# Two-layer hybrid attention kernel: each query tile's scores, the transposes of the tile ahead of it and the value products as one row on TensorE, held in program order between the weight products

## The chip, the cores and the metric

One core of a Trainium2 chip runs the whole program; the other cores stay idle. The metric is the device time of one execution in microseconds. Times of runs below are medians; the trace comes from one profiled execution.

## The reference

Two layers of a diffusion backbone work on 256 latent tokens and 256 context tokens of width 1024, all in fp32:

```python
for l in range(DEPTH):
    x = x + 0.5 * m[2] * swiglu(modulate(x, ...), w1, w3, w2)          # and the same for the context h
    o_lat, o_ctx = mixer(modulate(x, ...), modulate(h, ...), w_in[l], ...)
    x = x + m[5] * (o_lat @ w_out[l])
    x = x + 0.5 * m[8] * swiglu(modulate(x, ...), ...)                 # context too, in layer 0 only
return rms_norm(x, final_g)
```

The mixer projects the input once and feeds three groups of heads: a gated linear recurrence in both directions (4 heads), a neighbourhood attention with a bias per head (6 heads), and a windowed attention with rotary positions and a sink per head (6 heads that share 2 key heads). Each attention is `softmax(q @ k.T * scale + bias) @ v` over 256 latent and 256 context keys. Context queries see the 256 context keys alone, and only layer 0 has them.

## The kernel before, in words

**Products.** Weights are split into a high and a low part (line 109 on ScalarE, line 110 on VectorE), and `mm3` (line 237) makes three matmuls of each 128x128 weight block: high by high, low by high, high by low, all recorded at line 227. Activations lie transposed, so a product has up to 512 columns (both token sets) in layer 0 and 256 (latent alone) for most of the last layer.

**Attention.** `attention` (line 891) runs over *units*: a head pair j and a tile of 128 queries qt. Layer 0 has 12 units for each of the two kinds ("na", the neighbourhood kind, and "sw", the windowed kind), six of them with 512 keys (qt 0 and 1) and six with 256; layer 1 has six units of 512 keys for each kind. A unit has three stages:

- `stage_s`: the scores of both heads on TensorE (line 915, tile s), then a softmax on the other engines: on VectorE bias and row minimum in one pass (line 938; for 256 keys a reduction, line 943), for sw the sink (line 946); on ScalarE the exponential with its sum (line 947) and for sw that of the sink (line 949); on VectorE the sum (950), its reciprocal (951) and the scaling of P (952).
- `stage_t`: per head, four (or two) 128x128 transposes of P on TensorE (line 960, tile pt) and one copy out of PSUM on ScalarE (line 964, tile ptsb).
- `stage_v`: for two units together, the value products on TensorE (line 981, tile ot). After the last unit of a head pair ot is split into o by both engines (lines 221 and 222).

The loop's step i traces the scores of unit i, the transposes of unit i-1, and on odd i from 3 the value products of units i-2 and i-3.

**Order of the work.** `mixer` weaves three generators by the share of a stated cost that each has used: the projections followed by `w_out` (stated 99), the recurrence (stated 170) and attention (stated 30). `w_out` makes 8 output blocks of five products (15 matmuls) from the first five o tiles, which the recurrence and na fill; `w_out_end` adds the three o tiles of sw. Each kind of attention yields 34.8 cost units in layer 0, so that after na alone the attention's share (34.8 of 30) is past all that the first generator reaches (99.3 of 99): the sw steps are traced behind all 120 matmuls of `w_out`. In layer 1 a kind yields 17.4 (0.58 of 30), while the first generator stands at 57.7 of 99 (0.58) where `w_out` begins and ends at 70.7 (0.71): there the sw steps are traced among the products of `w_out`. The traced order isn't the order on the engines: a list scheduler fills each engine's queue by priority among what it holds ready. Attention is traced under `EARLIER = -450`, a priority of earlier work, so its instructions may be placed ahead of products that were traced before them. In the kernel before, only the scores of a head pair's first tile are held, behind a mark in the projection that makes their q and k (`R.marks`), and the transposes behind the last scores traced. Each engine then works its queue strictly in the order it has been given.

Of the kernel before, what the change touches and what calls it, by code (L numbers as in the profile page):

```python
# [197 lines left out]
class Kern:  # L198
# [27 lines left out]
    def mmul(self, *args, **kw):  # L226
        ins = self.nc.tensor.matmul(*args, **kw)  # L227
        if self.pinned:
            self.tc.keep_in_program_order(ins)
        return ins  # L230
# [5 lines left out]

    def mm3(self, ps, whi, wlo, ahi, alo, start, stop):
        mmul = self.mmul
        mmul(ps, whi, ahi, start=start, stop=False)
        mmul(ps, wlo, ahi, start=False, stop=False)  # L240
        return mmul(ps, whi, alo, start=False, stop=stop)


    def plan(self):
# [646 lines left out]
    def attention(self, l, R, kind):  # L891

        nc = self.nc
        nqt = R.nq // 128
        units = [(j, qt) for j in range(3) for qt in range(nqt)]
        U = {}
        ots = {}
        last = []

        def mark(i):  # L900
            return 2 * units[i][0] + 2 if kind == "na" else 8 + units[i][0]

        def ready(i):
            return i >= len(units) or len(R.marks) > mark(i)

        def stage_s(i):

            j, qt = units[i]
            k0, nk = (0, TOK) if qt < 2 else (SEQ, SEQ)
            qs = slice(qt * 128, qt * 128 + 128)  # L910
            q, ks = R.q[kind][j], R.k[kind][j]
            pss = [self.aux("s") for _ in range(2)]
            for hh in range(2):
                hs = slice(hh * 64, hh * 64 + 64)
                ins = nc.tensor.matmul(pss[hh][:, 0:nk], q[hs, qs], ks[hh][hs, k0:k0 + nk], start=True, stop=True)  # L915
                if hh == 1:
                    self.tc.keep_in_program_order(ins)
                elif qt == 0:
                    self.behind(ins, R.marks[mark(i)])
            last.append(ins)  # L920
            for hh in range(2):
                softmax(i, hh, pss[hh])

        def softmax(i, hh, ps):
            j, qt = units[i]
            h = 2 * j + hh
            nk = TOK if qt < 2 else SEQ
            sm = self.small("sm", 32)
            nmx, tot, es, rs = (sm[:, c:c + 1] for c in range(4))
            P = self.half("P")  # L930
            if qt < 2:
                if kind == "na":
                    b = h * 2 + qt
                    bias = self.bias[:, b:13:12 - b, :]
                else:
                    bias = self.swb[:, qt:3:2 - qt, :]
                src = P
                nc.vector.tensor_tensor_reduce(out=src.rearrange("p (a b) -> p a b", a=2),  # L938
                                               in0=ps.rearrange("p (a b) -> p a b", a=2), in1=bias, scale=1.0,
                                               scalar=3e38, op0=OP.add, op1=OP.min, accum_out=nmx)  # L940
            else:
                src = ps
                nc.vector.tensor_reduce(nmx, ps[:, 0:nk], axis=AX.X, op=OP.min)
            if kind == "sw":
                sk = self.sink[:, l * 6 + h:l * 6 + h + 1]
                nc.vector.tensor_scalar(nmx, nmx, sk, None, op0=OP.min)
            nc.scalar.activation(P[:, 0:nk], src[:, 0:nk], AF.Exp, bias=nmx, scale=-1.0, accum_out=tot)
            if kind == "sw":
                nc.scalar.activation(es, sk, AF.Exp, bias=nmx, scale=-1.0)
                nc.vector.tensor_tensor(out=tot, in0=tot, in1=es, op=OP.add)  # L950
            nc.vector.reciprocal(rs, tot)
            nc.vector.tensor_scalar(P[:, 0:nk], P[:, 0:nk], rs, None, op0=OP.mult)
            U[i, hh] = P

        def stage_t(i, hh):
            nk = TOK if units[i][1] < 2 else SEQ
            P = U.pop((i, hh))
            ps = self.aux("pt")
            for c in range(nk // 128):
                ins = nc.tensor.transpose(ps[:, c * 128:c * 128 + 128], P[:, c * 128:c * 128 + 128], self.ident)  # L960
                if c == 0:
                    self.behind(ins, last[-1])
            pt = self.half("ptsb")
            nc.scalar.activation(pt[:, 0:nk], ps[:, 0:nk], AF.Copy)
            U[i, hh] = pt

        def stage_v(ii):

            first = True
            for i in ii:  # L970
                j, qt = units[i]
                k0, nk = (0, TOK) if qt < 2 else (SEQ, SEQ)
                pts = [U.pop((i, hh)) for hh in range(2)]
                if j not in ots:
                    ots[j] = self.mm("ot")
                for c in range(nk // 128):
                    tt = k0 // 128 + c
                    for hh in (1, 0):
                        h = 2 * j + hh
                        vc = (h * 64) if kind == "na" else 384 + (h // 3) * 64  # L980
                        ins = nc.tensor.matmul(ots[j][hh * 64:hh * 64 + 64, qt * 128:qt * 128 + 128],  # L981
                                               R.V[tt // 2][:, tt % 2, vc:vc + 64], pts[hh][:, c * 128:c * 128 + 128],
                                               start=c == 0, stop=c == nk // 128 - 1)
                        if not first:
                            self.tc.keep_in_program_order(ins)
                        first = False
            if max(units[i][1] for i in ii) == nqt - 1:
                n = R.nq
                o = self.slot([128, 2, 512], F32R, "o")
                self.split(o[:, 0, 0:n], o[:, 1, 0:n], ots.pop(j)[:, 0:n])  # L990
                R.o[(2 if kind == "na" else 5) + j] = o

        n = len(units)
        for i in range(n + 2):
            while not ready(i):
                yield None
            if i < n:
                stage_s(i)
                yield 1.0
            for hh in range(2):  # L1000
                if 0 <= i - 1 < n:
                    stage_t(i - 1, hh)
                    yield 0.5
            if i >= 3 and i % 2 == 1:
                stage_v((i - 2, i - 3))
                yield 1.8

    def w_out(self, l, R):
        n = R.nq
# [438 lines left out]
```

## Time and profile before

| | |
|---|---|
| runs of the kernel before | 1867.47 us median of 3 (1866.44 to 1868.5) |
| the profiled execution | 1867.86 us, of it 1866.0 us from the first to the last instruction |
| TensorE busy | 1825.9 us (98%) |
| VectorE busy | 1205.9 us (65%) |
| ScalarE busy | 717.3 us (38%) |
| granted TensorE clock, mean | 0.995 of full speed |
| chain that ended last | TensorE 91%, VectorE 4% |
| attention on TensorE | scores 144 records, transposes 240, value products 480 |

Times are us from the start of the span unless marked ns. A row of the timeline merges equal instructions that follow each other and ends, in brackets, with the time that the engine stood idle before it and whose result it waited for. Matmuls are pipelined: the step from one start to the next is the price, not the length that is shown. A fp32 matmul leaves two records, so "x32" value products are 16 of the program. Idle time of an engine that isn't the bottleneck costs nothing; idle time of TensorE here is time of the whole kernel.

### The profile page before, as it was taken

The page shows a single profiled execution, that of the slowest core. Times are in us where ns is not written, and L with a number is a line of the kernel's source. Part 1 is how long each engine was busy: PE and PEld are TensorE (multiplying, and loading weights), DVE is VectorE, ACT ScalarE, POOL GpSimd, SP SyncE. Part 2 cuts the span into 40 slices and gives each one's busy share as a digit, 9 for nine tenths or more (in the row PEclk, how much of TensorE's full clock was granted, in tenths as well). Part 3 has the DMA queues.
Part 4 walks back from the last instruction along what each step waited for, and adds up shares of the span by engine and source line. Part 5 has one row for each costly group of instructions (what it writes and reads, how often), then busy time and mean ns, then how long its engine had stood idle before and what let it go on. Part 6 is the DMA issues. An engine that isn't in the chain of part 4 may idle for free.

```text
span 1866.0 us, 27641 instructions
## 1 busy us (share of the span) xinstructions
PE 1825.9 (98%) x11071; PEld 1501.0 (80%) x11071; DVE 1205.9 (65%) x2225; ACT 717.3 (38%) x1210; POOL 123.5 (7%) x198
## 2 busy tenths in 40 slices
PE   7999999999999999999999999999999999999998
PEld 4777787789777679778778797777788977789998
DVE  4877577765864769666576685565534766677554
ACT  4422222245345665222322352132223634665443
POOL 0000000030400020000000200000001140020000
PEclk8999999999999999999999999999999999999999
DMA  9645546432211214446455334565432321246651
GB/s 350 218 158 177 171 153 201 153 132 68 69 38 43 90 32 162 157 149 210 140 166 169 119 120 152 172 211 159 147 96 85 116 66 41 67 144 202 205 170 57
DMA packets 233641, 258.23 MB, mean 138 GB/s; under 512 B 18886, under 2 KB 195370, under 8 KB 233258
## 3 DMA queue, kind: packets, MB, share of 16 engines
q1 hardware_dynamic: 233514, 256.48, 43.0%
q8 instruction: 87, 1.43, 0.3%
q14 instruction: 40, 0.33, 0.1%
HBM read 255.41 MB, written 2.48 MB: 138 GB/s over the span
## 4 chain that ended last, share of the span: by engine, by line
PE 91%; DVE 4%; ACT 1%; POOL 1%; issue 1%; DMA 0%; SPq 0%; DVEq 0%; ACTq 0%; POOLq 0%
PE mm L227 83%; PE s L915 2%; PE ot L981 2%; PE pt L960 1%; PE adaps L377 1%; DVE P L938 1%; DVE wlo L110 1%; POOL k L793 1%; PE lv L766 0%; PE adaps L227 0%; PE adap L384 0%; POOL ssq L1294 0%; PE hgo L856 0%; DMA xraw<-in_ctx_dram 0%; DVE tot L800 0%
## 5 line engine op out<-in xcount | busy, mean ns | idle before, releaser
L227 PE MATMUL mm<-h,whi 128*128 128x512 f32 (+1 forms) x3264 | 909.6, 363 | 3.3 <-ACT h L1362 1.8
L227 PEld LDWEIGHTS mm<-h,whi 128*128 128x128 f32 x3264 | 581.1, 188 | 114.6 <-issue 8.2
L227 PE MATMUL mm<-h,wlo 128*128 128x512 f32 (+1 forms) x1632 | 588.4, 361 | 0.5 <-DVE wlo L110 0.5
L109 ACT ACTIVATE whi<-raw 128x1024 fp32r<-128x1024 f32 (+2 forms) x344 | 338.6, 1012 | 301.0 <-PE mm L227 197.4
L110 DVE TENSOR_TENSOR wlo<-raw,whi 128x1024 fp32r<-128x1024 f32 (+2 forms) x344 | 400.9, 1183 | 78.7 <-ACT whi L109 62.9
L227 PE MATMUL mm<-g,whi 128*128 128x512 f32 (+1 forms) x1480 | 402.4, 357 | 0.0
L227 PEld LDWEIGHTS mm<-h,wlo 128*128 128x128 f32 x1632 | 307.5, 188 | 49.8 <-DVE wlo L110 1.0
L367 DVE SCALAR_TENSOR_TENSOR adaacc<-adaraw,s,adaacc 128x512 f32<-128x512 f32 x392 | 274.7, 745 | 39.8 <-DMA adaraw<-in_ada_w_dram 38.8
L227 PEld LDWEIGHTS mm<-g,whi 128*128 128x128 f32 x1480 | 261.8, 188 | 47.4 <-ACT whi L109 4.2
L227 PE MATMUL mm<-g,wlo 128*128 128x512 f32 (+1 forms) x740 | 263.5, 356 | 0.0
L557 DVE TENSOR_TENSOR silu<-mm,silu 128x512 f32<-128x512 f32 (+1 forms) x80 | 49.5, 627 | 200.3 <-PE mm L227 135.2
L221 ACT ACTIVATE g<-silu 128x512 fp32r<-128x512 f32 (+1 forms) x92 | 51.3, 562 | 288.9 <-DVE silu L557 259.6
L433 DVE SCALAR_TENSOR_TENSOR xT<-mm,mod,xT 128x256 f32<-128x256 f32 x216 | 96.7, 478 | 100.1 <-PE mm L227 99.8
L227 PEld LDWEIGHTS mm<-g,wlo 128*128 128x128 f32 x740 | 139.1, 188 | 21.8
L1312 POOL CAST hp<-mod 128x2 fp32r<-128x2 f32 x40 | 21.8, 575 | 1274.8 <-PE mm L227 492.0
L556 ACT ACTIVATE silu<-mm 128x512 f32<-128x512 f32 (+1 forms) x80 | 42.9, 548 | 139.9 <-PE mm L227 139.9
L227 PE MATMUL mm<-hp,whi 128*128 128x258 f32 x384 | 73.7, 287 | 0.6 <-DVE xT L433 0.3
L222 DVE TENSOR_TENSOR g<-silu,g 128x512 fp32r<-128x512 f32 (+1 forms) x92 | 54.5, 602 | 29.9 <-ACT g L221 29.4
L227 PE MATMUL mm<-o,whi 128*128 128x256 f32 (+1 forms) x280 | 67.9, 331 | 0.0
L227 PE MATMUL mm<-whi,h 128*128 128x256 f32 (+1 forms) x256 | 65.9, 350 | 0.4 <-ACT k L640 0.4
L1294 POOL TENSOR_TENSOR ssq<-ssq,sq 128x256 f32<-128x256 f32 x50 | 44.3, 898 | 293.3 <-ACT sq L1291 293.1
L227 PEld LDWEIGHTS mm<-hp,whi 128*128 128x128 f32 x384 | 60.8, 190 | 1.1 <-ACT whi L109 0.6
(197 smaller groups left out, 1498.8 us busy)
## 6 DMA issues: line engine op xcount, KB each, us to landing
raw<-in_ffn_w_dram SPq DMA_DIRECT2D x120, 1024.0 KB, 5.4
adaraw<-in_ada_w_dram SPq DMA_DIRECT2D x144, 512.0 KB, 5.2
raw<-in_ffn_w_dram SPq DMA_DIRECT2D x16, 768.0 KB, 4.5
raw<-in_w_in_dram SPq DMA_DIRECT2D x12, 1024.0 KB, 5.1
raw<-in_w_in_dram SPq DMA_DIRECT2D x16, 512.0 KB, 5.1
raw<-in_w_out_dram SPq DMA_DIRECT2D x8, 640.0 KB, 3.9
bias<-scr SPq DMA_DIRECT2D x48, 64.0 KB, 3.4
raw<-in_w_in_dram SPq DMA_DIRECT2D x4, 768.0 KB, 4.6
```

Source lines behind the costliest of these rows:

```text
L109: for ins in (K.nc.scalar.activation(hi, v, AF.Copy), K.nc.vector.tensor_tensor(out=lo, in0=v, in1=hi.bitcast(F32), op=OP.subtract)):
L110: K.nc.vector.tensor_tensor(out=lo, in0=v, in1=hi.bitcast(F32), op=OP.subtract)):
L221: self.nc.scalar.activation(hi, src, AF.Copy)
L222: self.nc.vector.tensor_tensor(out=lo, in0=src, in1=hi.bitcast(F32), op=OP.subtract)
L227: ins = self.nc.tensor.matmul(*args, **kw)
L367: nc.vector.scalar_tensor_tensor(acc[:, t], w, sc, acc[:, t], op0=OP.mult, op1=OP.add)
L433: self.nc.vector.scalar_tensor_tensor(self.x[:, d, sl], ps[:, sl], self.mod[l][:, m, d, s:s + 1], self.x[:, d, sl], op0=OP.mult, op1=OP.add)
L556: nc.scalar.activation(a[:, 0:n], ps[i][:, 0:n], AF.Silu)
L557: nc.vector.tensor_tensor(out=a[:, 0:n], in0=ps[2 + i][:, 0:n], in1=a[:, 0:n], op=OP.mult)
L915: ins = nc.tensor.matmul(pss[hh][:, 0:nk], q[hs, qs], ks[hh][hs, k0:k0 + nk], start=True, stop=True)
L981: ins = nc.tensor.matmul(ots[j][hh * 64:hh * 64 + 64, qt * 128:qt * 128 + 128], R.V[tt // 2][:, tt % 2, vc:vc + 64], pts[hh][:, c * 128:c ...
L1294: eng.tensor_tensor(out=self.ssq[s], in0=self.ssq[s], in1=t, op=OP.add)
```

## The change

`mm3` remembers the last matmul of each product (`self.product`). The scores of every unit, no longer those of a head pair's first tile alone, are placed behind the product that was traced last. Within one step of the loop the second head's scores, all transposes and all value products are kept in program order, the first transpose behind the scores. At the end of the step the last of them is remembered (`self.row_end`), and the first matmul of the next product is placed behind it. The step yields once, 2.0 on even i and 3.8 on odd i, at the loop's ends too, where a stage is missing: a kind now yields 40.6 in layer 0 (34.8 before) and 23.2 in layer 1 (17.4 before), and 23.2 of 30 (0.77) is past the 0.71 at which layer 1's `w_out` ends, so that there, too, the sw steps are now traced behind all of `w_out`. No arithmetic, tile, pool or transfer changes.

```diff
     def mm3(self, ps, whi, wlo, ahi, alo, start, stop):
         mmul = self.mmul
-        mmul(ps, whi, ahi, start=start, stop=False)
+        ins = mmul(ps, whi, ahi, start=start, stop=False)
+        if self.row_end is not None:
+            self.behind(ins, self.row_end)
+            self.row_end = None
         mmul(ps, wlo, ahi, start=False, stop=False)
-        return mmul(ps, whi, alo, start=False, stop=stop)
+        self.product = mmul(ps, whi, alo, start=False, stop=stop)
+        return self.product
...
                 if hh == 1:
                     self.tc.keep_in_program_order(ins)
-                elif qt == 0:
-                    self.behind(ins, R.marks[mark(i)])
+                else:
+                    self.behind(ins, self.product)
...
                 ins = nc.tensor.transpose(ps[:, c * 128:c * 128 + 128], P[:, c * 128:c * 128 + 128], self.ident)
-                if c == 0:
+                if c == 0 and hh == 0:
                     self.behind(ins, last[-1])
+                self.tc.keep_in_program_order(ins)
+            last.append(ins)
...
-                        if not first:
-                            self.tc.keep_in_program_order(ins)
-                        first = False
+                        self.tc.keep_in_program_order(ins)
+            last.append(ins)
...
             if i < n:
                 stage_s(i)
-                yield 1.0
-            for hh in range(2):
-                if 0 <= i - 1 < n:
+            if 0 <= i - 1 < n:
+                for hh in range(2):
                     stage_t(i - 1, hh)
-                    yield 0.5
             if i >= 3 and i % 2 == 1:
                 stage_v((i - 2, i - 3))
-                yield 1.8
+            self.row_end = last[-1]
+            yield 2.0 if i % 2 == 0 else 3.8
```

What this does to the queues is shown at three places. In these listings s, pt and ot are the tiles of scores, transposes and value products, `mm<-h` a product of a projection, `mm<-o` one of `w_out`, and line numbers of the changed kernel are 7 or 8 higher (scores at 922, transposes at 967, value products at 989, the exponential at 954, the copy of pt at 973).

TensorE, layer 0, the beginning of the windowed attention, before:

```order
L227 MATMUL mm<-o,whi 128x512
L227 MATMUL mm<-o,wlo 128x512
L227 MATMUL mm<-o,whi 128x512 x2
L227 MATMUL mm<-o,wlo 128x512
L960 MATMUL pt<-cc,P 128x128 x4
L227 MATMUL mm<-o,whi 128x512 x2
L227 MATMUL mm<-o,wlo 128x512
L227 MATMUL mm<-o,whi 128x512
L960 MATMUL pt<-cc,P 128x128 x4
L915 MATMUL s<-sqk 128x256
L915 MATMUL s<-swap,sqk 128x256
L960 MATMUL pt<-cc,P 128x128 x4
```

The same place with the change:

```order
L227 MATMUL mm<-o,whi 128x512
L922 MATMUL s<-sqk 128x512
L922 MATMUL s<-swap,sqk 128x512
L922 MATMUL s<-sqk 128x512
L922 MATMUL s<-swap,sqk 128x512
L967 MATMUL pt<-cc,P 128x128 x8
L922 MATMUL s<-sqk 128x256
L922 MATMUL s<-swap,sqk 128x256
L967 MATMUL pt<-cc,P 128x128 x8
L922 MATMUL s<-sqk 128x256
L922 MATMUL s<-swap,sqk 128x256
L967 MATMUL pt<-cc,P 128x128 x4
```

All 120 matmuls of `w_out`'s products now stand ahead of the first of these scores, and from there to the last value product all 12 rows of the windowed attention follow each other with no product between; the six rows of layer 1 do the same.

TensorE, layer 0, the first rows of the neighbourhood attention, before:

```order
L915 MATMUL s<-nqk 128x512 x4
L227 MATMUL mm<-h,whi 128x512
L227 MATMUL mm<-h,wlo 128x512
L227 MATMUL mm<-h,whi 128x512 x2
L227 MATMUL mm<-h,wlo 128x512
L227 MATMUL mm<-h,whi 128x512 x2
L960 MATMUL pt<-cc,P 128x128 x8
```

The same place with the change:

```order
L922 MATMUL s<-nqk 128x512 x4
L967 MATMUL pt<-cc,P 128x128 x8
L922 MATMUL s<-nqk 128x256 x2
L967 MATMUL pt<-cc,P 128x128 x8
```

The seven matmuls of products between the scores of the first two units and the first transposes are gone from there; they now stand behind the value products.

ScalarE with the change, layer 0, a pair of units with 512 keys inside the windowed attention (P is the exponential, sm that of the sink, ptsb the copy of the transposes):

```order
L973 ACTIVATE ptsb<-pt 128x512
L954 ACTIVATE P,sm<-P,sm 128x512
L956 ACTIVATE sm<-sink,sm 128x1
L954 ACTIVATE P,sm<-P,sm 128x512
L956 ACTIVATE sm<-sink,sm 128x1
L973 ACTIVATE ptsb<-pt 128x512
```

The copy in the first row belongs to the earlier unit of the pair, the four rows behind it to the softmax of the later one: it stands queued behind that copy, which in turn needs the earlier unit's transposes.

## Rows read from the trace of the kernel before

**Rows 1.** The page, busy time of the engine (us, share of the span, instructions).
```profile
PE 1825.9 (98%) x11071; PEld 1501.0 (80%) x11071; DVE 1205.9 (65%) x2225; ACT 717.3 (38%) x1210; POOL 123.5 (7%) x198
```
**Rows 2.** Busy time by stretch, both windowed attentions: PE, PEld, DVE, ACT, POOL, clock, DMA.
```profile
615.70:677.30 61.60, 60.12 (x377) 40.60 (x376) 41.90 (x151) 37.19 (x103) 0.61 (x4) 1.00 0.22 69
1619.80:1653.50 33.70, 31.43 (x269) 24.97 (x268) 25.68 (x90) 23.13 (x56) 0.61 (x4) 1.00 0.35 108
```
**Rows 3.** The same stretches, matmuls of line 227 alone: PE, PEld, clock, DMA.
```profile
615.70:677.30 61.60, 31.55 (x116) 20.73 (x116) 1.00 0.22 69
1619.80:1653.50 33.70, 14.06 (x100) 12.37 (x100) 1.00 0.35 108
```
**Rows 4.** Timeline of TensorE, neighbourhood attention without products between: start, length, instruction.
```profile
606.53 1.13 PE L915 MATMUL s<-nqk 64*128 64x512 f32 x4
607.59 1.09 PE L960 MATMUL pt<-cc,P 128*128 128x128 f32 x8
608.62 1.14 PE L915 MATMUL s<-nqk 64*128 64x256 f32 x4
610.10 0.63 PE L960 MATMUL pt<-cc,P 128*128 128x128 f32 x4 [0.35 <-DVE P L952]
611.36 0.63 PE L960 MATMUL pt<-cc,P 128*128 128x128 f32 x4 [0.63 <-ACT P L947]
611.91 0.70 PE L915 MATMUL s<-nqk 64*128 64x256 f32 x4
612.55 0.74 PE L960 MATMUL pt<-cc,P 128*128 128x128 f32 x4
613.22 1.97 PE L981 MATMUL ot<-ptsb,v 128*64 128x128 f32 x32
615.12 0.66 PE L960 MATMUL pt<-cc,P 128*128 128x128 f32 x4
615.70 1.12 PE L915 MATMUL s<-sqk 64*128 64x512 f32 x2
```
**Rows 5.** Timeline of TensorE, products alone, layer 0.
```profile
646.29 0.62 PE L227 MATMUL mm<-o,whi 128*128 128x512 f32 x2
...
646.99 0.64 PE L227 MATMUL mm<-o,whi 128*128 128x512 f32 x2
```
**Rows 6.** Timeline of VectorE: steps of the softmax of units with 512 keys.
```profile
609.27 0.16 DVE L951 RECIPROCAL sm<-sm 128x1 f32<-128x1 f32 x1 [0.27 <-ACT P L947]
609.47 0.49 DVE L952 TENSOR_SCALAR P<-P,sm 128x512 f32<-128x512 f32 x1
...
616.86 0.69 DVE L938 CUSTOM_DVE_ANT_1 P<-s,cc 128x512 f32<-128x512 f32 x1 [2.15 <-PE s L915]
...
622.91 0.16 DVE L950 TENSOR_TENSOR sm<-sm 128x1 f32<-128x1 f32 x1
...
623.11 0.16 DVE L951 RECIPROCAL sm<-sm 128x1 f32<-128x1 f32 x1
```
**Rows 7.** Timeline of ScalarE: exponentials and a copy of transposes, 512 keys.
```profile
617.85 0.72 ACT L947 ACTIVATE P<-P,sm 128x512 f32<-128x512 f32 x1 [1.60 <-DVE sm L946]
...
621.88 0.72 ACT L947 ACTIVATE P<-P,sm 128x512 f32<-128x512 f32 x1 [0.35 <-DVE sm L946]
...
622.79 0.58 ACT L964 ACTIVATE ptsb<-pt 128x512 f32<-128x512 f32 x1
```
**Rows 8.** Timeline of TensorE: first transposes of the neighbourhood attention, layers 0 and 1.
```profile
528.90 1.22 PE L960 MATMUL pt<-cc,P 128*128 128x128 f32 x8 [0.62 <-DVE sm L951]
...
1560.74 0.63 PE L960 MATMUL pt<-cc,P 128*128 128x128 f32 x4 [1.31 <-DVE P L952]
```
**Rows 9.** Busy time by stretch around a fall of the granted clock, as in rows 2.
```profile
1528.20:1531.60 3.40, 1.40 (x15) 0.86 (x17) 2.92 (x7) 1.11 (x3) 3.40 (x5) 1.00 1.05 291
1531.70:1535.10 3.40, 3.40 (x33) 2.25 (x29) 1.69 (x7) 0.00 (x0) 1.34 (x3) 0.50 0.00 0
```
**Rows 10.** Timeline of TensorE, the wait in the first of those stretches.
```profile
1531.45 0.54 PE L766 MATMUL lv<-q,klev 64*64 64x64 f32 x16 [2.00 <-DVE q L793]
```

More of the change, by code (lines that the diff above doesn't have):

```diff
@@ L238, in mm3 @@
         mmul = self.mmul
-        mmul(ps, whi, ahi, start=start, stop=False)
+        ins = mmul(ps, whi, ahi, start=start, stop=False)
+        if self.row_end is not None:
+            self.behind(ins, self.row_end)
+            self.row_end = None
         mmul(ps, wlo, ahi, start=False, stop=False)
-        return mmul(ps, whi, alo, start=False, stop=stop)
+        self.product = mmul(ps, whi, alo, start=False, stop=stop)
+        return self.product
+    product = None
+    row_end = None
     def plan(self):
@@ L967, in stage_v @@
         def stage_v(ii):
-            first = True
             for i in ii:
```

## The prediction

> **What bounds the kernel now.** I read the busy times first: TensorE works 98% of the span, so the time moves with what its queue holds and with the stretches in which it waits [rows 1]. Then busy time by stretch, for the two places that the change rearranges most, the windowed attention of both layers: in 61.6 us of layer 0 TensorE stands idle 61.60 - 60.12 = 1.5 us, in 33.7 us of layer 1 33.70 - 31.43 = 2.3 us, while VectorE and ScalarE are busy for two thirds or more of both [rows 2]. The reader should see that the softmax chains, long as they are, cost almost nothing there, because products of `w_out` lie between: 116 and 100 of their matmuls [rows 3]. Third, TensorE's timeline where attention already stands without products: it shows the price of a row and that waits appear at once, 0.35 and 0.63 us ahead of two groups of transposes [rows 4].
>
> **What the change does to the queues.** Scores can no longer be pulled ahead of products. In both layers all products of `w_out` now come first, and then 12 (layer 0) and 6 (layer 1) rows of windowed attention in one block. The work is the same; what changes is the price of fragments and, above all, what covers the softmax.
>
> *TensorE's own work.* A row of 512 keys costs 606.53 to 607.59 = 1.06 us for scores, 607.59 to 608.62 = 1.03 for transposes, and half of 613.22 to 615.12, 0.95, for value products: 3.04. A row of 256 keys costs 0.64 (611.91 to 612.55), 0.58 (615.12 to 615.70) and, half of 0.95, 0.48, with a step into another kind of matmul 0.51: 1.73 [rows 4]. Six of each in layer 0: 18.2 + 10.4 = 28.6; six long ones in layer 1: 18.2. Three matmuls of a product take 646.29 to 646.99 = 0.70 us, 0.233 each [rows 5]; with 256 columns I take half, 0.117 (their mean busy time, 14.06/100 = 0.14, bounds it from above [rows 3]). The products are 116 x 0.233 = 27.1 and 100 x 0.117 = 11.7. All that: 85.6 us. Before, the same work with its waits took 61.6 less about 1.0 for value products of the other kind (32 records take 1.90, these are half as many [rows 4]), and 33.7: 94.3. So the block saves 94.3 - 85.6 = 8.7 us: 3.8 of waits and some 5 of scattered fragments (a lone head's scores cost as much as a pair's).
>
> *The new waits.* From a long unit's scores to its transposes: 615.70 to 616.86 = 1.16 until VectorE begins [rows 4, 6]; 616.86 to 617.85 = 0.99 to the exponential; 621.88 to 622.91 = 1.03 to the sum; 622.91 to 623.11 and 609.27 to 609.47 = 0.20 + 0.20 to the scaling; 609.47 to 610.10 = 0.63 to the first transpose [rows 4, 6, 7]. Sum 4.2 us; the second head is 0.9 behind, the time of one exponential and its companions on ScalarE (621.88 to 622.79 [rows 7]).
>
> - First pair of a block: scores of two units, then nothing to do. With two heads of each queued on VectorE the first transposes come some 5.4 after the first scores and find 2.0 us of cover: 3.4, with 0.2 to 0.3 between the heads 3.6.
> - A later pair of long units: the even one has its own scores, the transposes of the unit ahead and the next scores as cover, 3.0 of 4.2, so it waits 1.2, and 0.4 for its second head. The odd one has value products as well, 4.9, and would not wait; but ScalarE's queue holds its exponentials behind the copy of the even unit's transposes. They begin only after that, which puts up to two exponentials (1.8) back onto the path. 1.6 to 3.4; I take 3.4, since that order is in the queue.
> - A pair of short units: the same steps with half the columns, about 3.0 of latency against 2.3 of cover, 0.7, and 0.3 for the second head: 1.0, with the same delay at the halved length (0.6) 1.6.
> - End of a block: the last value products wait for the copy of the last transposes, 0.6 to 0.8 (its length is 0.58 [rows 7]).
>
> Layer 0 has one first, two later and three short pairs: 3.6 + 2 x 3.4 + 3 x 1.6 + 0.6 = 15.8. Layer 1: 3.6 + 2 x 3.4 + 0.8 = 11.2. Together 27.0. Bounds: with the lower values 10.4 + 7.6 = 18.0; if every pair pays half as much again because odd units wait like even ones (5.0 long, 3.0 short), 23.2 + 14.4 = 37.6.
>
> *The neighbourhood attention.* Its rows keep products between them in most places. In layer 0 the first transposes lose seven matmuls of cover, 7 x 0.233 = 1.6, on top of the 0.62 that they wait now; in layer 1 five short ones go from a place that already waits 1.31 [rows 8], with the second head 0.9. Two rows of layer 1 now follow directly on others: 4.2 less 0.6 for the missing sink steps against 3.0 of cover, 0.4 for the second head and 0.6 for a copy, 1.6 each, less 1.0 of waits that they have now: 2.2. Sum 1.6 + 0.9 + 2.2 = 4.7, say 5, between 2 and 8. Matmuls that left these places run later at the same price.
>
> *The clock.* The trace has one wait of 2.00 us in mid-kernel [rows 10]. Behind a stretch in which TensorE was busy 1.40 of 3.40 us, the granted clock is 0.50, that is 1.2 GHz, for the whole of the next stretch, though TensorE is busy throughout, before it is 2.4 GHz again [rows 9]. That costs half of 3.4 us, 1.7, where products run. The changed blocks begin with waits of 3.4 us, so I expect the same behind each, once more behind a later pair, and once behind the neighbourhood attention's first wait of 2.2: four falls at 1.5, because slow scores also fill some of the wait, 6 us. Lower bound 0; upper bound, both blocks wholly at half clock: 28.6 + 18.2 = 46.8 us of work twice as long, less about 14 of the waits that it then covers, 33. The Trainium skill, "TensorE: Matmul & The Clock Gate", section "HAM oscillation — how this bites in real kernels", says that when waits recur between short bursts of matmuls, the array falls to its lower clock in each and every burst begins slow. By that rule, with one fall behind each of the nine pairs at 1.5, the clock would cost 13.5 instead of 6 and the time be 1905; rows 9 and 10 agree on a single wait, and no run here shows recurring ones.
>
> *Nothing else.* SP's queue, transfers and buffers are untouched. `w_out`'s products now run without attention between them, in layer 1 in 120 x 0.117 = 14 us; weights are covered if their conversions keep ahead as they do now, which I cost at nothing; a late one would add some 2 us.
>
> **Sum.** -8.7 + 27.0 + 4.7 + 6 = +29.0 on the profiled execution's 1867.86 us, 0.4 above the median of the runs: 1897.
>
> **The rivals.**
>
> - *No fall of the clock:* the waits break up into pieces shorter than the one that brought a fall. For it: attention-dense stretches run at 1.00 now [rows 2]. Against: the first wait of each block is longer than the one that brought a fall. 1867.9 - 8.7 + 27.0 + 4.7 = 1891.
> - *Half clock through both blocks:* the waits inside keep it down. For it: one 2-us wait sufficed. Against: at half clock TensorE waits less, and in rows 9 a busy stretch brought it back. 1891 + 33 = 1924.
> - *Longer waits:* odd units wait like even ones. For it: the queue order on ScalarE. 37.6 for 27.0, with the clock's 6: 1908.
> - *Faster:* softmax of one unit hides behind the work of its neighbours, as in the rows without products of the neighbourhood attention, 0.35 + 0.63 = 1.0 us for four units [rows 4]. For 18 units that is 4.4 in place of 8.7 saved, and 0 elsewhere: 1867.9 - 8.7 + 4.4 = 1864. It decides where waits in the two blocks stay under 8.7 us, half a microsecond a unit. Against: three of those four units have 256 keys and the first was prepared before; the sink adds 0.6 to the chain.
> - *No effect:* the blocks are not executed as queued. TensorE's queue is strictly ordered, so I leave it little: 1868.
>
> **How the numbers follow.** Forecast as it stands 0.55; no fall 0.20; half clock throughout 0.10; longer waits 0.08; faster 0.04; no effect 0.03. The range must take in forecast, no fall and longer waits with the bounds of their terms. Low: waits of 18.0, no fall, 1867.9 - 8.7 + 18.0 + 4.7 = 1882; I begin at 1884. High: it stops just under the half-clock case, 1922. Left out: most of that case, faster and no effect, under 0.2. 0.2% (3.7 us) is about what a measurement of this kernel tells from no change. Faster by more than that 0.04; within it, 0.02, the greater part of "no effect"; slower 0.94.
>
> **What would show it.** In the changed profile TensorE's busy share falls to some 97%. The transposes' row shows some 30 us of idle time in front of it instead of a few, released by the scaling and sums on VectorE. Busy time by stretch finds a block of about 44 us in layer 0 and 29 in layer 1 with no matmul of line 227, TensorE's work in them near 28.6 and 18.2, and a granted clock under 1 in part of each. Wrong would be: products inside those blocks; waits under 9 us in all; a clock of 1.00 throughout; or growth outside the two mixers, whose other parts should keep their times.

## The result and the profile after

The changed kernel takes 1893.97 us (median of 4 executions, 1889.93 to 1894.03) beside 1867.7 us of the kernel before (4 executions, 1866.44 to 1868.5): a ratio of 1.014, 95% interval 1.0128 to 1.0152, 26.3 us slower. The profiled execution took 1889.93 us with a span of 1888.1 us; it is the fastest of the four and has the highest mean granted clock, 0.993 against 0.989 to 0.990.

The page's line of busy times, as [rows 1]:

```profile
PE 1828.7 (97%) x11071; PEld 1504.2 (80%) x11071; DVE 1213.2 (64%) x2225; ACT 713.1 (38%) x1206; POOL 123.5 (7%) x198
```

TensorE is busy for 2.8 us more than before, the span is 22.1 us longer: TensorE stands still. The list of its waits says for what (waiting line, releasing line: us in total, times, longest):

```profile
PE pt L967 <- DVE sm L957: 6.5, 2, 3.4
PE pt L967 <- DVE P L959: 6.3, 8, 1.1
...
PE pt L967 <- DVE sm L958: 3.5, 2, 2.4
...
PE pt L967 <- DVE sm L953: 3.0, 4, 1.3
...
PE ot L989 <- ACT ptsb L973: 2.0, 3, 0.7
PE pt L967 <- ACT ptsb L973: 1.6, 3, 0.7
```

The rows shown are transposes and value products that wait for softmax steps or copies; the waits left out belong mostly to other stages and are about as long before. Ahead of all transposes together TensorE waits 22.4 us, 7.3 before. Busy time by stretch shows where: the two windowed attentions, first all instructions (PE, PEld, DVE, ACT, POOL, clock, DMA), as [rows 2], then line 227 alone (PE, PEld, clock, DMA), as [rows 3]:

```profile
645.80:691.00 45.20, 35.17 (x273) 20.52 (x272) 33.13 (x136) 31.91 (x101) 0.00 (x0) 1.00 0.01 1
1644.50:1677.30 32.80, 24.48 (x169) 16.36 (x168) 19.69 (x75) 18.45 (x50) 0.00 (x0) 0.84 0.11 34
```

```profile
645.80:691.00 45.20, 0.13 (x1) 0.00 (x0) 1.00 0.01 1
1644.50:1677.30 32.80, 0.04 (x1) 0.00 (x0) 0.84 0.11 34
```

The products are gone from both; 45.20 - 35.17 = 10.0 us and 32.80 - 24.48 = 8.3 us stand open, where [rows 2] had 1.5 and 2.3. Layer 0 in the timeline of TensorE (start, length, instruction, idle time before it):

```profile
650.89 0.63 PE L967 MATMUL pt<-cc,P 128*128 128x128 f32 x4 [3.05 <-DVE sm L957]
651.86 0.63 PE L967 MATMUL pt<-cc,P 128*128 128x128 f32 x4 [0.35 <-DVE P L959]
...
661.23 1.98 PE L922 MATMUL s<-sqk 64*128 64x512 f32 x4 [0.20 <-DVE sm L945]
...
668.76 0.63 PE L967 MATMUL pt<-cc,P 128*128 128x128 f32 x4 [1.01 <-DVE P L959]
669.32 1.43 PE L922 MATMUL s<-sqk 64*128 64x256 f32 x4
```

The first pair of units waits 3.4 us, later ones 1.2 to 1.5. Two rows hide more: scores that took 1.13 and 0.70 us in [rows 4] take 1.98 and 1.43. Their second head waits for one of the four PSUM buffers that scores and transposes share (e12 below, with more buffers, has no such rows); the merged row shows that as length, not as idle time. Five such places cost 0.67 + 2 x 0.92 + 2 x 0.77 = 4.0 us.

Layer 1, the same place, and the granted clock (0.50 is 1.2 GHz) in three of its stretches:

```profile
1649.88 1.92 PE L967 MATMUL pt<-cc,P 128*128 128x128 f32 x8 [3.42 <-DVE sm L957]
1651.72 1.90 PE L922 MATMUL s<-sqk 64*128 64x512 f32 x4
...
1659.07 0.63 PE L967 MATMUL pt<-cc,P 128*128 128x128 f32 x4 [1.26 <-DVE sm L953]
1659.63 3.23 PE L989 MATMUL ot<-ptsb,v 128*64 128x128 f32 x32
```

```profile
1649.90:1653.30 3.40, 3.40 (x12) 1.91 (x12) 2.02 (x8) 1.57 (x5) 0.00 (x0) 0.50 0.00 0
...
1660.10:1663.50 3.40, 3.40 (x30) 2.86 (x28) 1.36 (x5) 1.20 (x5) 0.00 (x0) 0.51 0.00 0
1673.80:1677.20 3.40, 3.26 (x31) 3.26 (x32) 0.00 (x0) 0.09 (x1) 0.00 (x0) 0.50 0.00 0
```

Behind the 3.42 us wait everything costs up to twice as much: eight transposes 1.92 for 1.09, 32 value products 3.23 for 1.97 [rows 4]. In layer 0 the wait is 3.05 us and the clock stays 1.00.

### The profile page after: what moved, and what is told of

Read it like the earlier page. It is cut to its first block, busy times and chain, and to the rows that moved or that the text cites. A ratio compares the mean times of both kernels' runs of the same rounds, so it can differ in the third digit from the quotient of the medians.

```text
span 1888.1 us, 27635 instructions
## 1 busy us (share of the span) xinstructions
PE 1828.7 (97%) x11071; PEld 1504.2 (80%) x11071; DVE 1213.2 (64%) x2225; ACT 713.1 (38%) x1206; POOL 123.5 (7%) x198
## 3 DMA queue, kind: packets, MB, share of 16 engines
q8 instruction: 87, 1.43, 0.3%
## 4 chain that ended last, share of the span: by engine, by line
PE 90%; DVE 5%; ACT 2%; issue 1%; POOL 1%; DMA 0%; SPq 0%; DVEq 0%; ACTq 0%; POOLq 0%
PE mm L227 82%; PE ot L989 2%; PE s L922 1%; PE pt L967 1%; DVE P L945 1%; PE adaps L384 1%; DVE wlo L110 1%; ACT P L954 1%; POOL k L800 1%; PE lv L773 0%; DVE P L959 0%; PE adaps L227 0%; PE adap L391 0%; PE hgo L863 0%; DVE tot L807 0%
## 5 line engine op out<-in xcount | busy, mean ns | idle before, releaser
L967 PEld LDWEIGHTS pt<-cc,P 128*128 128x128 f32 x240 | 25.9, 143 | 46.9 <-issue 20.8
```

## The experiments

The theory: binding scores behind the last traced product takes away the products that covered the softmax, at once in layer 0 and, with the new yields, in layer 1; falls of the clock come on top. Rivals: the order inside a row, the products held back behind a row, PSUM buffers, the spacing alone. Each ratio is to the kernel before, run on the same chip beside it (medians 1867.3 to 1867.9 us).

| run | edit | median us | ratio, 95% interval |
|---|---|---|---|
| e1 | scores' binding undone | 1874.17 | 1.0038 (1.0023 to 1.0052) |
| e2 | binding of the next product undone | 1888.96 | 1.0112 (1.0097 to 1.0127) |
| e3 | yields undone | 1884.02 | 1.0089 (1.0074 to 1.0104) |
| e4 | attention stated at 81 | 1888.56 | 1.0114 (1.0097 to 1.0131) |
| e5 | even yields | 1865.43 | 0.9989 (0.9980 to 0.9998) |
| e6 | even yields, next product free | 1859.74 | 0.9959 (0.9946 to 0.9971) |
| e7 | transposes two units behind | 1887.37 | 1.0106 (1.0092 to 1.0120) |
| e8 | idle work in the waits | 1887.49 | 1.0105 (1.0090 to 1.0121) |
| e9 | kernel before and scores' binding | 1878.89 | 1.0066 (1.0052 to 1.0080) |
| e10 | kernel before and order in a row | 1867.03 | 0.9997 (0.9988 to 1.0006) |
| e11 | kernel before with even yields | 1866.61 | 0.9998 (0.9989 to 1.0007) |
| e12 | e7 and more PSUM | 1887.61 | 1.0108 (1.0094 to 1.0121) |

### One part undone: e1, e2, e3

```diff
-                else:
-                    self.behind(ins, self.product)
+                elif qt == 0:
+                    self.behind(ins, R.marks[mark(i)])
```

> One binding undone: a unit's scores are no longer placed behind the product traced last, only the first tile of a head pair behind its mark, as before the change. Rows stay in program order inside, the next product stays behind the row traced last, yields stay. In the queue the rows of the windowed attention then stand among the products of w_out again in both layers. Theory (the scores' binding took the products away that covered the softmax): 1864 to 1872 us, TensorE's waits in the two windowed attentions back under 5 us, and no half clock there. Rival (order inside a row, or the binding of the next product behind a row, is what costs): 1885 to 1894 us, waits at the transposes still 15 us or more.

1874.17 us: 19.8 of the 26.3 us are back, 6.9 stay, so above the range given. There is no half clock in the two windowed attentions, and the waits there are 1.4 and 2.8 us.

```diff
-        ins = mmul(ps, whi, ahi, start=start, stop=False)
-        if self.row_end is not None:
-            self.behind(ins, self.row_end)
-            self.row_end = None
+        mmul(ps, whi, ahi, start=start, stop=False)
```

> The other binding undone: the first product behind a row is free again, the scores stay bound. In the queue the windowed attention remains a block without products in both layers (nothing is traced behind it that could move up), while the neighbourhood attention gets seven of its products back between the first scores and the first transposes. Theory: only the neighbourhood attention's term returns, 2 to 6 us, so 1888 to 1892 us. Rival (products held back behind rows are the main cost): 1866 to 1875 us.

1888.96 us, as the theory said. The first transposes of the neighbourhood attention in layer 0, with the change and in this run (the latter as in [rows 8]):

```profile
527.89 1.22 PE L967 MATMUL pt<-cc,P 128*128 128x128 f32 x8 [2.45 <-DVE sm L958]
```

```profile
528.43 1.22 PE L964 MATMUL pt<-cc,P 128*128 128x128 f32 x8 [0.62 <-DVE sm L955]
```

```diff
-            yield 2.0 if i % 2 == 0 else 3.8
+            yield (1.0 if i < n else 0.0) + (1.0 if 0 <= i - 1 < n else 0.0) + (1.8 if i >= 3 and i % 2 == 1 else 0.0)
```

> Only the stated cost of attention goes back to the old amounts (17.4 a kind in layer 1, 34.8 in layer 0); both bindings stay. Layer 0's windowed attention remains one block behind all products of w_out; in layer 1 products of w_out stand between its first rows (30, 60 and 30 matmuls) and the later rows follow each other. Theory: layer 0 keeps its loss of 9 us, layer 1 gets back 4 to 9 of its 13 us, so 1885 to 1890 us; no wait of over 2 us ahead of layer 1's first transposes of this attention. Rival (the place among the traced products does not matter, only the bindings do): 1892 to 1895 us.

1884.02 us, 10.0 back, 1.0 more than the range allowed. Layer 1's first transposes of the windowed attention find products ahead of them (only the second head waits), and its clock is 1.00 throughout:

```profile
1639.44 0.66 PE L967 MATMUL pt<-cc,P 128*128 128x128 f32 x4
1640.51 0.63 PE L967 MATMUL pt<-cc,P 128*128 128x128 f32 x4 [0.41 <-DVE P L959]
```

### One part alone: e9, e10

```diff
-                elif qt == 0:
-                    self.behind(ins, R.marks[mark(i)])
+                else:
+                    self.behind(ins, self.product)
```

> The kernel before with one part of the change alone: the scores of every unit stand behind the product traced last. Order inside a row, the next product behind a row and the yields are as before. In the queue layer 0's windowed attention is again one block behind all 120 matmuls of w_out; layer 1's first rows keep 24 to 60 matmuls between them and the rest follow each other. Theory (this binding carries the loss of layer 0, and with the yields that of layer 1): 9 us lost in layer 0 and 3 to 5 in layer 1, so 1878 to 1885 us, near the run with the old yields. Rival (the binding costs only together with the fixed order of a row): 1867 to 1872 us.

1878.89 us: the scores' binding alone costs 11.4 us, without any of the row's order. Layer 0 is a block again; after 3.04 us of waiting its eight transposes take 2.06 us:

```profile
648.03 2.06 PE L963 MATMUL pt<-cc,P 128*128 128x128 f32 x8 [3.04 <-DVE sm L953]
```

e10 leaves both bindings and the new yields out of the changed kernel, that is, the edits of e1, e2 and e3 together.

> The part of the change that is left without its two bindings and with the old yields: second head's scores, transposes and value products of a step in program order, nothing else. In the queue products stand among the rows as before. Theory (this order costs nothing as long as products lie between): 1865 to 1870 us. Rival (the order itself costs, which would be the 6.9 us that stayed when the scores' binding was undone): 1872 us or more.

1867.03 us, ratio 0.9997 (0.9988 to 1.0006): the order inside a row costs nothing. What e1 left, 6.9 us, belongs to the other binding and the yields.

### Cover given back: e4, e5, e6, e11

```diff
-              (hg(), 170.0), (att(), 30.0))
+              (hg(), 170.0), (att(), 81.0))
```

> Both bindings and the new yields stay, but attention is stated to the planner at 81 instead of 30, so that its rows are traced among the products of w_out (windowed attention) and of the projections (neighbourhood attention) instead of behind all of them. No other change. Theory (rows are only dear when nothing covers their softmax; with a product or more between two rows the fixed row costs no more than the scheduler's own order): 1862 to 1872 us, blocks without matmuls of line 227 gone, waits under 10 us. Rival A (the fixed order of a row is dear wherever it stands): 1885 us or more. Rival B (the time comes out well under the kernel before because whole rows save fragments): under 1862 us.

1888.56 us: missed. The rows came too early and still in bunches. The first scores of the windowed attention stand right behind the projection and wait for q; four units stand there without a product between:

```profile
611.34 0.67 PE L922 MATMUL s<-sqk 64*128 64x512 f32 x1 [1.07 <-DVE sqk L747]
...
616.34 2.04 PE L967 MATMUL pt<-cc,P 128*128 128x128 f32 x8 [3.02 <-DVE sm L957]
```

By the time alone rival A would stand; the rows show that this edit did not test it, since the cover was still missing. So the next run set the spacing itself:

```diff
+        share = {("na", 12): 19.0, ("sw", 12): 7.0, ("na", 6): 13.0, ("sw", 6): 3.2}[kind, n]
         for i in range(n + 2):
...
-            yield 2.0 if i % 2 == 0 else 3.8
+            yield share / n
```

> Both bindings and the rows stay as in the change; only what attention yields to the planner is new: equal amounts per step, 19 and 13 (layers 0 and 1) in all for the neighbourhood kind, 7 and 3.2 for the windowed kind. In the queue each of the 12 windowed rows of layer 0 now stands behind 9 matmuls of w_out, in layer 1 behind 12 to 18. Nine matmuls are 9 x 0.233 = 2.1 us, so the cover of a row's softmax is 5.1 us against the 4.2 to 5.1 that it takes. Theory (missing cover is the cause, not the fixed order): waits inside the two windowed stretches under 3 us in all, no fall of the clock there, and the stretches save up to 6 us on the kernel before (its 3.8 us of waits and some fragments), less 3 us for the neighbourhood attention: 1863 to 1869 us. Rival (the fixed order of a row is dear wherever it stands): 1880 us or more.

1865.43 us. Same bindings, same rows, 28.5 us less than the change. e6 is e5 with the edit of e2:

> As the run with even yields, and in addition the first product behind a row is free again. In the queue the neighbourhood attention's first pairs of both layers get 7 and 12 matmuls of products between scores and transposes; the windowed rows stay evenly spread. Theory: another 2 to 4 us, the first wait of the neighbourhood attention in layer 0 (2.4 us) back to 0.6: 1860 to 1866 us, which would be under the kernel before. Rival (free products only break up rows and cost fragments): no better than the run with even yields.

1859.74 us, 8.1 under the kernel before, the fastest of all and 0.3 under its range. The windowed attentions of e6 by stretch, all instructions and, for layer 0, line 227 alone:

```profile
615.10:675.30 60.20, 58.80 (x390) 39.53 (x390) 44.58 (x158) 37.61 (x109) 0.61 (x4) 1.00 0.14 47
1611.30:1647.90 36.60, 34.47 (x297) 27.80 (x297) 28.94 (x94) 24.27 (x59) 1.80 (x4) 1.00 0.24 76
```

```profile
615.10:675.30 60.20, 31.36 (x117) 20.74 (x118) 1.00 0.14 47
```

Waits of 1.4 and 2.1 us, clock 1.00, 117 products' matmuls among the rows. e11 gives the same yields to the kernel before, once a step, without any binding of the change:

> The kernel before with the even yields of the fastest run (19 and 13 for the neighbourhood kind, 7 and 3.2 for the windowed kind, once a step) and none of the change's bindings or orders: the scheduler may still pull scores ahead. It tells what the spacing is worth by itself. Theory (spacing gives the cover, the scores' binding only keeps it): 1861 to 1866 us, 1 to 6 us slower than the fastest run because rows are broken up again. Rival (all of the gain is spacing): 1859 to 1861 us.

1866.61 us: the spacing alone is worth nothing measurable, and the run is 0.6 us above its range. The page's busy times of e6 and of e11 tell the two apart:

```profile
PE 1819.8 (98%) x11071; PEld 1498.8 (81%) x11071; DVE 1211.0 (65%) x2225; ACT 713.9 (38%) x1208; POOL 125.2 (7%) x198
```

```profile
PE 1827.0 (98%) x11071; PEld 1500.6 (80%) x11071; DVE 1208.3 (65%) x2225; ACT 714.5 (38%) x1208; POOL 124.3 (7%) x198
```

With the bindings TensorE has 7.2 us less to do, about the whole difference in time (6.9); up to 1.7 of it is a half-clock stretch in mid-kernel that e6's profiled execution lacks. Where the scheduler is free it parts the heads of a unit, as here in e11:

```profile
624.36 0.70 PE L915 MATMUL s<-sqk 64*128 64x256 f32 x2
624.98 0.51 PE L227 MATMUL mm<-o,whi 128*128 128x512 f32 x1
625.42 0.70 PE L915 MATMUL s<-swap,sqk 64*128 64x256 f32 x2
626.04 0.51 PE L227 MATMUL mm<-o,whi 128*128 128x512 f32 x1
```

Each head costs 0.62 us (624.36 to 624.98, 625.42 to 626.04); the pair costs 0.64 [rows 4]. How much of the 7.2 us the scores' binding carries and how much the order inside a row was not separated; the order alone, without the even yields, gained nothing measurable (e10).

### The clock: e8

```diff
+            if kind == "sw" and i in (1, 3, 5):
+                ps = self.mm("fill")
+                for c in range(22 if i == 1 else 6):
+                    ins = nc.tensor.transpose(ps[:, c % 4 * 128:c % 4 * 128 + 128], self.ident, self.ident)
+                    if c == 0:
+                        self.behind(ins, last[-1])
+                    self.tc.keep_in_program_order(ins)
             if 0 <= i - 1 < n:
```

> The change with idle work added on TensorE: 22 transposes of the constant identity (about 2.8 us) ahead of the first transposes of each windowed block and 6 (0.7 us) ahead of those of units 2 and 4, into a tile that nobody reads; all else stays. They lie in waits of 3.0 to 3.4 and about 1 us, so without an effect on the clock the time would stay at 1894 or rise by at most 1 us. Theory (falls of the clock behind these waits cost some 5 to 8 us): fewer falls in the two blocks and 1886 to 1891 us. Rival (the clock does not matter here): 1893 to 1896 us.

1887.49 us: work that nobody needs makes the kernel 6.5 us faster. Start of layer 1's block, and both blocks by stretch:

```profile
1648.74 2.62 PE L1009 MATMUL fill<-cc 128*128 128x128 f32 x22
1652.24 0.63 PE L967 MATMUL pt<-cc,P 128*128 128x128 f32 x4 [0.87 <-DVE sm L957]
```

```profile
645.80:691.00 45.20, 38.91 (x307) 24.23 (x306) 33.16 (x136) 31.83 (x101) 0.00 (x0) 1.00 0.00 1
1646.80:1674.60 27.80, 24.30 (x204) 16.40 (x203) 19.72 (x75) 18.39 (x50) 0.00 (x0) 1.00 0.13 40
```

The transposes still start 3.4 us after the last scores. But layer 1's block shrinks from 32.80 to 27.80 us at clock 1.00, so its three half-clock stretches had cost 5.0, 1.7 each. Layer 0's block is as long as it was, because in the change's profiled execution it had no fall. The other three executions of the change took 4 us more at a lower mean clock; further falls, in layer 0 for instance, fit, but no profile of them shows that.

Nor is e8's profiled execution free of half clock elsewhere. One stretch of it, at 710.6 us, comes after a wait of 1.38 us in a later stage, another after the mid-kernel wait of [rows 10]. The change waits as long at both places, and its profiled execution has no half clock from 38 to 1649 us. The second place, e8 and then the change, TensorE's wait and the clock behind it:

```profile
1542.03 0.46 PE L773 MATMUL lv<-q,klev 64*64 64x64 f32 x16 [2.01 <-DVE q L800]
1543.60:1547.00 3.40, 3.40 (x24) 2.24 (x23) 1.25 (x6) 0.00 (x0) 0.01 (x1) 0.50 0.02 5
```

```profile
1541.11 0.46 PE L773 MATMUL lv<-q,klev 64*64 64x64 f32 x16 [2.01 <-DVE q L800]
1541.50:1544.90 3.40, 3.40 (x34) 2.58 (x29) 2.44 (x10) 0.00 (x0) 1.20 (x2) 1.00 0.02 5
```

So e8's profiled execution, at 1887.15 us, is only 2.8 us under the change's, and of the 6.5 us between the medians the profiles place 5.0, in layer 1's block; where the rest comes from stays open.

### A deeper row instead of products: e7, e12

```diff
+        lag = 2 if kind == "sw" else 1
...
-            if 0 <= i - 1 < n:
+            if 0 <= i - lag < n:
                 for hh in range(2):
-                    stage_t(i - 1, hh)
+                    stage_t(i - lag, hh)
```

Value products come one step later accordingly.

> The change with one thing altered, in the windowed attention only: a row holds the scores of unit i, the transposes of unit i-2 (not i-1) and value products one step later. The blocks without products stay. Between a unit's scores and its transposes now lie two rows of other attention work, some 5 to 6 us, against 4.2 to 5.1 of softmax. Theory (cover is what is missing, and the block's own work is 28.6 and 18.2 us): waits in the blocks only at their first transposes (2.4 us instead of 3.4) and at the end; both blocks together 10 to 14 us shorter and few falls of the clock: 1878 to 1885 us. Rival (the 4 PSUM buffers or ScalarE's and VectorE's queues limit the block, 24 us of exponentials and copies at two thirds busy): under 4 us gained, 1890 us or more.

1887.37 us: 6.6 better than the change, short of the range. In layer 1, where all units have 512 keys, the idle time falls from 8.3 to 3.9 us (25.00 - 21.06):

```profile
1648.80:1673.80 25.00, 21.06 (x170) 13.26 (x168) 18.75 (x75) 17.90 (x50) 0.00 (x0) 0.93 0.14 44
```

In layer 0 the block is no shorter, 46.8 us, with two stretches at half clock in it. e12 tried the PSUM buffers:

```diff
-            pss = [self.aux("s") for _ in range(2)]
+            pss = [self.aux("s") if kind == "na" or hh == 0 else self.mm("s") for hh in range(2)]
```

> The run with transposes two units behind, and in addition the second head's scores of the windowed attention in the other PSUM pool, the one of the products, which stands nearly empty there; the order on TensorE is the same. Theory (in layer 0 the scores of units with 256 keys hold their PSUM buffer until their exponential is done, and the next scores wait for it): waits and stretched scores in layer 0's block down by 3 to 6 us and the time 1881 to 1885 us. Rival (the buffers are not what limits, VectorE and ScalarE are): 1886 to 1888 us as without.

1887.61 us, as the rival said: the stretched scores are gone, but the transposes wait instead. At the block's end both runs meet something new, here in e12, ScalarE and then TensorE:

```profile
680.08 1.28 ACT L616 ACT_TABLE_LOAD   x1
681.38 0.20 ACT L616 ACTIVATE preload<-eps 128x1 f32<-128x1 f32 x1
681.58 1.28 ACT L954 ACT_TABLE_LOAD   x1
```

```profile
684.65 3.54 PE L989 MATMUL ot<-ptsb,v 128*64 128x128 f32 x32 [4.28 <-ACT ptsb L973]
```

A function table meant for the next stage is loaded ahead of the last exponentials, and theirs again: 2.8 us, on the path where no products cover it. How much of the rest of layer 0 is VectorE's queue and how much ScalarE's was not separated.

## Why the prediction was right

The time was forecast at 1897 us and came at 1893.97. The mechanism of the likeliest case is the one that the runs show: products gone from between the rows, waits for the softmax, and falls of the clock on top. That the sum came within 3 us of the time owes something to luck, since misses of single terms offset each other.

- **Products gone, two blocks.** Right: no product in 45.2 and 32.8 us (said: 44 and 29). e9 shows the scores' binding to be enough for layer 0, e3 that layer 1 needs the new yields too, and e1 that these yields without the scores' binding make no block. Binding and yields were both named as the cause.
- **TensorE's own work, -8.7.** Nearly: layer 0's block has 35.17 busy less 1.0 of another stage's matmuls and 4.0 of stretched scores, 30.1 us (said 28.6). Layer 1's, added up step by step from e8's timeline at full clock without idle time, fills and stretched rows, is 18.4 (said 18.2). The gain from whole rows is real: e6 has 7.2 us less work on TensorE than e11, of which at most 1.7 is the clock. What the products themselves cost in the change, part of the -8.7, was not measured.
- **New waits, 27.0.** Oversized by 3.6 us: layer 0 has 10.0 + 4.0 = 14.0 (said 15.8), layer 1 27.8 - 18.4 = 9.4 (said 11.2). The sign named for it, some 30 us of idle time ahead of the transposes, came at 22.4, because part of the waits is hidden in stretched rows and ahead of value products. First pairs fit well: 3.05 + 0.35 for 3.6. A later long pair of layer 0 cost 0.20 + 0.46 + 0.55 open and 0.92 stretched, 2.1, not the 3.4 that I took: the exponentials held behind a copy did not add two full lengths. PSUM buffers as a limit were missed: "buffers are untouched" was true, and wrong as a reason to cost them at nothing.
- **Neighbourhood attention, 4.7.** About right in all, not in its parts. From the first neighbourhood scores to the first windowed ones, TensorE's idle time ahead of attention's instructions grew from 1.80 to 4.65 us in layer 0 (2.9, said 1.6; its first wait from 0.62 to 2.45) and from 2.25 to 3.38 in layer 1 (1.1, said 0.9 + 2.2): 4.0 in all. Layer 1's first wait, which was to grow by 0.9, was 1.31 [rows 8] and is 1.10 with the change (at 1568.85 us). Freeing the next product (e2) shortens these stretches from 122.4 to 120.0 and from 80.5 to 79.1 us, 3.8 together.
- **The clock, 6.** Near in size, not in place. e8 returns 6.5, 5.0 of which a profile shows. In the profiled execution three falls stand in layer 1 and none in layer 0 or behind the neighbourhood attention's first wait, so the sign "a granted clock under 1 in part of each" held for layer 1 alone. The step behind it, that a wait at least as long as the 2.00 us of [rows 10] brings a fall, came from one example, and the runs do not bear it out: that very wait was followed by half clock in the kernel before and in e8, not in the change. The rule cited from the Trainium skill, "TensorE: Matmul & The Clock Gate", section "HAM oscillation — how this bites in real kernels", would have had a fall behind each of nine pairs and 13.5 us. The trace agrees with it only in part: falls recur in layer 1, three of them, and in layer 0 there are none. The example in that section of the Trainium skill has longer waits between its bursts than the later pairs here, so that nine falls stretched the rule.
- **The rivals.** "No fall" (1891) is as near to the median as the forecast, and nearer to the profiled execution (1889.93): the time alone could not tell the two apart, the 0.50 rows do. "Half clock throughout" (1924), "faster" (1864) and "no effect" did not happen; the gain of the faster rival is there only when products lie between rows (e5, e6).

Terms as measured, -7.0 (own work 1.5 and 0.2 above what was said), 23.4 for waits, 4.0 and 6.5, sum to 26.9 against 26.3. But 6.5 is a difference of medians, while the other terms come from profiled executions, which lie 22.1 us apart. With the 5.0 that the profiles show for the clock, and 1.7 taken off because the change's has no fall behind the wait of [rows 10], the terms give 23.7: 1.6 us stay unexplained.

## What to carry to other kernels

Before binding work in program order, look at what lies between producer and consumer in the queue afterwards: in this kernel the bound rows of attention were cheaper on TensorE than scattered ones (e6 against e11), but only with 2 us or so of other work between rows to cover a softmax of an estimated 4 to 5 us. So set the order and the spacing together: the same bindings cost 26 us with the change's yields, gain 2 with even ones (e5) and, one of them dropped, 8 (e6). Where a wait of TensorE can't be covered by useful work, try idle matmuls in it (e8: 6.5 us less).

## What the chip showed that was not expected

- Waits of equal length may or may not be followed by half clock. The mid-kernel wait of 2.0 us was in the kernel before [rows 9, 10] and in e8, and was not in the change. At the start of layer 0's windowed attention 3.05 us were not (the change) and 3.04 us were (e9); the neighbourhood attention's 2.45 us were not in the change, and were in e5. What decides between the two, no run here shows. The stretch in e5 (the clock is the third number from the end):

```profile
528.80:532.20 3.40, 3.40 (x17) 2.43 (x16) 2.16 (x9) 2.07 (x6) 0.00 (x0) 0.61 0.00 0
```

- A wait for a PSUM buffer inside a merged group of scores shows as a longer group, 1.98 us for 1.13, and not as idle time; part of the block's loss is invisible in the list of waits.
- Two loads of ScalarE's function tables, 1.28 us each, stand in layer 0 of the kernel before too (674.23 and 675.74), under the products; in a block without products 4.28 us of waiting stand behind them (e12).
